# A two-layer trunk kernel whose list scheduler gets other delays and another plan for the front parts

## The chip, the cores and the metric

The kernel runs on one core of one Trainium2 chip. The metric is the device time of one execution in microseconds (us). The engines of the core are TensorE (PE in the profile), VectorE (DVE), ScalarE (ACT), GpSimd (POOL) and SyncE (SP). SyncE only issues transfers (DMAs); POOL issues some too.

## The reference, cut to what matters

Sequence length 512, model width 1024, two layers, everything in float32:

```python
h = x @ w_in[l]                                  # 1024 -> q | k | v | u, 512 each
q, k, v, u = jnp.split(h, splits, axis=-1)
attn_out = diff_attention(q, k, v, lam, ...)     # rotary, 4 heads, two softmaxes each, p0 - lam * p1, RMSNorm per head
ssm_out = s5_ssm(u, ...)                         # 32 groups of 16 channels, 64 complex states each, GELU, GLU
mix = jnp.concatenate([attn_out, ssm_out], axis=-1) @ w_out[l]
x = layer_norm(ALPHA * x + mix, ln1_g[l], ln1_b[l])
ff = jnp.square(jax.nn.relu(x @ w_ff1[l])) @ w_ff2[l]    # 1024 -> 4096 -> 1024
x = layer_norm(ALPHA * x + ff, ln2_g[l], ln2_b[l])
```

## The kernel before, in words

**Products.** Every float32 product is three products in a faster format (`mm3`): both factors are split in a high part and the rest, and high x high, high x low and low x high are added up in PSUM. A weight tile of 128 x 1024 comes by DMA into `raw`; `whi` is a ScalarE cast of it, `wlo` the difference `raw - whi`. Who makes `wlo` is chosen by a letter in `PLAN` (lines 42 to 85): V is one VectorE subtraction, P one GpSimd subtraction, A a ScalarE activation with scale -1 and then a DMA from POOL's queue that adds `raw` on its way. The strings are `lo` (projections, one letter per tile in the order of `back`), `flo` (first feed-forward matrix), `nlo` (out-projection), `glo` (second feed-forward matrix) and `elo` (the last feed-forward block). There are four buffers of `whi` and of `wlo` and five of `raw`.

**Stages, with their time in the profiled execution.** The front of layer 0 (0 to some 216 us) holds the projections (groups `0q0` to `0q3`, `0k0`.., `0v0`.., `0u0`..), four attention heads of four row blocks (`0a00` to `0a33`, each head finished in `0e0` to `0e3`), the state-space model in four quarters (`0ssm_pars`, `_load`, `_a`, `_b`, `_c`, `_outp`) and the GLU (`0g0` to `0g3`). The out-projection and LayerNorm follow, then the feed-forward loop (267 to 556 us). Layer 1 has the same: its front from 556 to 780, its loop from 820 to 1117, and the last block with the store up to the end. The tables of layer 1's state-space model are made inside layer 0.

**Part-height copies.** The input of the state-space model is spread over partitions with 16 ScalarE copies of 32 x 128 per quarter (`u<-ps_acc`), its output matrices with 32-row copies too (`mx<-m`). q and k go through ScalarE casts of 64 x 512 (`xq<-rt`) and four 32-row DMAs for the rotary halves (`rt<-rt`).

**The feed-forward loop.** Each of seven blocks runs `f m1 m7 f m2 m4 f m6 f m5 m3`: `f` is a tile of the first matrix (24 products of 512 columns, then on ScalarE the ReLU `rt`, on VectorE the square, into `y` or `mh`), m1 to m7 are the seven products of a Strassen-like scheme over the second matrix (12 products each, in two PSUM banks `ps_sc`; VectorE adds each bank into `xq` or `rt`). m5 and m3 share their two banks, so m3's first product into a bank waits until m5's result was added from it. The eighth block (`ffend`) is an ordinary product.

**What sets the order.** The kernel first records all instructions (`Rec.add`), with their dependences. `cost` says how long each holds its engine, `lat` how much later one that depends on it can start. `run` is a list scheduler: it simulates the engines and at each step takes, on the engine that is free first, the ready instruction with the smallest `prio`, which is minus the longest path to the end (`rank`) minus an offset. The offsets come from stage knobs (`ao`, `ap` for attention, `so`, `sp` for the state-space model, `po` for layer 1's tables) and from the table `pri`, two numbers per group, the first for all engines but TensorE and the second for TensorE. Where the simulated TensorE would idle for more than 500 ns ahead of an attention head's work, `fill` puts filler products of 256 columns on a constant (`ps_sc<-wz`), whose result is never read. At the end `issue` emits everything in planned order, so all instructions of the profile have one line, L506. The chip then runs each engine's list in that order, whatever the true durations are.

Of the kernel before, what the change touches and what calls it, by code (L numbers as in the profile page):

```python
# [14 lines left out]
F32R = mybir.dt.float32r  # L15
# [5 lines left out]
P = 128  # L21
# [22 lines left out]
        "q0 u0 k0 u1 v0 u2 v1 q1 k1 u3 q2 v2 k2 v3 q3 k3 g0 g1 g2 g3".split(),  # L44
        "u0 k0 u2 q0 u1 v0 v1 q1 k1 u3 v2 q2 k2 v3 q3 k3 g0 g1 g2 g3".split(),
    ],
    "att": [[8, 11, 14, 18], [8, 12, 15, 18]],
    "s5": [[4, 14], [3, 13]],
    "bufs": {"slot": 13, "mh": 2, "y": 3, "xq": 13, "at": 4, "rt": 5, "u": 4},
    "ps": {"acc": 2, "sc": 4, "s5": 2},  # L50
    "lo": ["AAAVAAPAAAAVAAAAAAAA", "AAAAAAAAAAAAAAAVAAVA"],
    "eng": {"rope": ["VVV", "VVV"], "tab": ["VVVVVV", "VVVVVV"], "cg": ["VVVV", "VVPV"], "ch": ["VVVV", "VVVV"], "sa": ["PV", "VP"], "sb": ["VVVVVV", "VVVVVV"]},
    "flo": "AVVV",
    "nlo": "APVAVPPV",
    "glo": "VPPPAPV",
    "seq": "f m1 m7 f m2 m4 f m6 f m5 m3",
    "elo": "VVVV",
    "wb": 4,
    "s5o": "p1 p0 o0 a0 b0 a1 c0 p2 o1 b1 a2 c1 b2 p3 a3 o2 b3 c2 o3 c3",
    "swq": "S",  # L60
    "ao": [-6000, 4000],
    "so": [2000, 19000],
    "ap": [40500, 56750],
    "sp": [31000, 27000],
    "pw": -6000,
    "smk": 2,
    "raw": 5,
# [110 lines left out]
class Rec:  # L178
# [181 lines left out]
    def run(self):  # L360
# [4 lines left out]
        todo, rel, wait = {}, {}, {}  # L365
# [26 lines left out]
        while len(order) < len(self.ops):  # L392
            best = None
            for e in engs:
                if ready[e]:
                    t = free[e]
                elif future[e]:
                    t = max(free[e], future[e][0][0])
# [6 lines left out]
            t, e = best  # L405
# [27 lines left out]
            if op.port:  # L433
                t = max(t, port["POOL" if e == "DVE" else "DVE"])
# [4 lines left out]
            if e == "PE" and t - pe_end > PLAN["gap"][1]:  # L439
                n = self.fill(pe_end, t, warm, live, extra)  # L440
# [1228 lines left out]
```

## Time and profile before

| | |
|---|---|
| median of 3 timed runs | 1150.72 us (1150.34 to 1151.69) |
| the profiled execution | 1151.48 us, of which the profile's span is 1149.7 |
| mean granted TensorE clock | 0.997 of full |
| TensorE busy | 1117.1 us, 97% |
| VectorE busy | 912.5 us, 79% |
| ScalarE busy | 632.2 us, 55% |
| GpSimd busy | 260.3 us, 23% |

Times within the trace are us from the start of the span. A figure in brackets behind an instruction is the idle time of its engine ahead of it and what ended that.

### The profile page before, as it was taken

What the parts mean: (1) busy time and instruction counts of PE and PEld (TensorE: products, weight loads), DVE (VectorE), ACT (ScalarE), POOL (GpSimd) and SP (SyncE); (2) the same over time, 40 slices, a digit from 0 to 9 for tenths busy, and PEclk for the clock granted to TensorE, in tenths of its full rate; (3) what the DMA queues carried; (4) which work ended last, traced back from release to release, by engine and by line L of the source; (5) the groups of instructions that cost most, each with busy time, mean ns of one, the idle gap of its engine ahead of it and who ended that gap; (6) DMA issues with size and microseconds to landing.
All of it is one profiled execution on the core that took longest, in us unless ns stands there. A gap on an engine that the chain in (4) does not pass through costs nothing.

```text
span 1149.7 us, 16190 instructions
## 1 busy us (share of the span) xinstructions
PE 1117.1 (97%) x5840; PEld 936.0 (81%) x5840; DVE 912.5 (79%) x1569; ACT 632.2 (55%) x1202; POOL 260.3 (23%) x198
## 2 busy tenths in 40 slices
PE   9999999999999999999999999999999999999997
PEld 7778877889888888888788878878988888888885
DVE  7898998887778878767792988867777778778788
ACT  7886869425544464444537788873454445445440
POOL 1011110311232242133021221022032143133221
PEclk9999999999999999999999999999999999999999
DMA  9443642441562452553678662652444454355231
GB/s 320 101 119 75 156 121 65 157 135 58 147 155 86 129 168 86 147 147 99 197 202 216 173 169 63 191 155 79 137 139 123 134 128 129 110 147 129 91 110 74
DMA packets 50960, 154.12 MB, mean 134 GB/s; under 512 B 6848, under 2 KB 7104, under 8 KB 50880
## 3 DMA queue, kind: packets, MB, share of 16 engines
q1 hardware_dynamic: 42240, 121.63, 32.6%
q0 software_dynamic: 8640, 31.46, 15.3%
q8 instruction: 46, 0.75, 0.3%
q14 instruction: 34, 0.28, 0.1%
HBM read 110.07 MB, written 7.34 MB: 102 GB/s over the span
## 4 chain that ended last, share of the span: by engine, by line
PE 66%; ACT 5%; DVE 2%; issue 2%; DMA 1%; SPq 0%; DVEq 0%; ACTq 0%; POOLq 0%
PE ps_acc L506 35%; PE ps_sc L506 23%; PE ps_s L506 8%; ACT whi L506 1%; ACT u L506 1%; DVE xq L506 1%; DVE wlo L506 1%; ACT at L506 1%; ACT wlo L506 1%; DMA wlo<-raw 0%; DMA keep<-xq 0%; ACT xq L506 0%; ACT xTh L506 0%; DVE xTl L506 0%; DMA xq<-xs 0%
## 5 line engine op out<-in xcount | busy, mean ns | idle before, releaser
L506 ACT CAST whi<-raw 128x1024 fp32r<-128x1024 f32 x222 | 232.2, 1051 | 264.2 <-PE ps_acc L506 129.4
L506 PE MATMUL ps_acc<-xTh,whi 128*128 128x512 f32 (+1 forms) x712 | 268.9, 379 | 4.6 <-ACT u L506 3.7
L506 PE MATMUL ps_acc<-xTl,whi 128*128 128x512 f32 (+1 forms) x712 | 268.3, 378 | 1.7 <-DVE xTl L506 1.3
L506 PE MATMUL ps_acc<-xTh,wlo 128*128 128x512 f32 (+1 forms) x712 | 268.0, 378 | 0.0
L506 PE MATMUL ps_sc<-whi,slot 128*128 128x512 f32 x784 | 254.5, 391 | 1.2 <-DVE xq L506 0.6
L506 POOL TENSOR_TENSOR wlo<-raw,whi 128x1024 fp32r<-128x1024 f32 x62 | 156.2, 2519 | 418.7 <-ACT whi L506 410.9
L506 PEld LDWEIGHTS ps_sc<-whi,slot 128*128 128x128 f32 x784 | 147.0, 188 | 34.6 <-issue 4.1
L506 DVE TENSOR_TENSOR wlo<-raw,whi 128x1024 fp32r<-128x1024 f32 x100 | 122.0, 1221 | 47.1 <-ACT whi L506 47.0
L506 PEld LDWEIGHTS ps_acc<-xTh,whi 128*128 128x128 f32 x712 | 134.0, 188 | 29.3 <-ACT u L506 4.5
L506 PEld LDWEIGHTS ps_acc<-xTl,whi 128*128 128x128 f32 x712 | 134.1, 188 | 24.7 <-DVE xTl L506 1.9
L506 PE MATMUL ps_sc<-wlo,slot 128*128 128x512 f32 x392 | 153.0, 390 | 0.0
L506 PEld LDWEIGHTS ps_acc<-xTh,wlo 128*128 128x128 f32 x712 | 133.9, 188 | 22.9 <-DMA wlo<-raw 0.3
L506 DVE TENSOR_TENSOR slot<-slot 128x512 fp32r<-128x512 f32 (+4 forms) x143 | 126.5, 893 | 6.5 <-ACT slot L506 6.0
L506 POOL DMA_DIRECT2D wlo<-raw x60 | 53.0, 887 | 231.5 <-ACT wlo L506 114.6
L506 ACT ACTIVATE wlo<-raw 128x1024 fp32r<-128x1024 f32 x60 | 63.4, 1059 | 61.9 <-PE ps_s L506 32.4
L506 PEld LDWEIGHTS ps_sc<-wlo,slot 128*128 128x128 f32 x392 | 73.6, 188 | 14.7
L506 DVE TENSOR_TENSOR xq<-xq,ps_sc 128x512 f32<-128x512 f32 x124 | 83.1, 679 | 0.7 <-PE ps_sc L506 0.7
L506 DVE TENSOR_TENSOR raw<-raw 128x1024 f32<-128x1024 f32 x56 | 68.4, 1221 | 0.6
L506 ACT CAST slot<-slot 128x512 fp32r<-128x512 f32 x56 | 34.5, 617 | 51.1 <-DVE slot L506 49.1
L506 PE MATMUL ps_acc<-whi,xTh 128*128 128x256 f32 (+1 forms) x176 | 56.4, 320 | 0.8 <-ACT u L506 0.7
L506 PE MATMUL ps_acc<-wlo,xTh 128*128 128x256 f32 (+1 forms) x176 | 55.9, 319 | 0.4 <-DVE wlo L506 0.4
L506 PE MATMUL ps_acc<-whi,xTl 128*128 128x256 f32 (+1 forms) x176 | 55.4, 318 | 0.0
(229 smaller groups left out, 1902.3 us busy)
## 6 DMA issues: line engine op xcount, KB each, us to landing
raw<-in_w_ff_dram SPq DMA_DIRECT2D x128, 512.0 KB, 3.5
wlo<-raw POOLq DMA_DIRECT2D x60, 512.0 KB, 5.3
raw<-in_w_qk_dram SPq DMA_DIRECT2D x16, 512.0 KB, 5.2
raw<-in_w_out_dram SPq DMA_DIRECT2D x16, 512.0 KB, 4.1
raw<-in_w_u_dram SPq DMA_DIRECT2D x8, 512.0 KB, 5.4
raw<-in_w_v_dram SPq DMA_DIRECT2D x8, 512.0 KB, 6.6
rt<-rt SPq DMA_DIRECT2D x64, 64.0 KB, 2.6
at<-in_ln_dram SPq DMA_DIRECT2D x16, 256.0 KB, 4.4
```

Of the source, the lines that this page charges most:

```text
L506: getattr(self.real[op.eng], op.name)(*[_real(x) for x in op.a], **{n: _real(x) for n, x in op.k.items()})
```

## The change

Two things. The numbers of `lat`, `cost` and `run` change: a ScalarE result is seen by POOL after 180 ns (395 when POOL issues a DMA on it) in place of 140; part-height copies cost 113 ns more on ScalarE and 105 more on VectorE; SP's DMAs hold the queue for 690 or 520 ns in place of 650 or 475; plain float32 products 10 ns of overhead in place of 5; products with an `xq` operand get a spacing of their own; `accum_out` on ScalarE 130 in place of 95; two GpSimd forms have new formulas; and ScalarE waits 80 ns after a buffer was released. And the plan changes: the letters of some low halves, the engine of a state-space combination of layer 1 (`cg`, one of four from GpSimd to VectorE), the stage knobs, and 71 of the 92 entries of `pri`, which gets 17 new ones (two of them are shown, the others read alike).

```diff
-    "att": [[8, 11, 14, 18], [8, 12, 15, 18]],
-    "s5": [[4, 14], [3, 13]],
+    "att": [[8, 12, 15, 19], [8, 12, 15, 18]],
+    "s5": [[4, 14], [6, 13]],
...
-    "eng": {..., "cg": ["VVVV", "VVPV"], ...},
+    "eng": {..., "cg": ["VVVV", "VVVV"], ...},
...
-    "nlo": "APVAVPPV",
-    "glo": "VPPPAPV",
+    "nlo": "APVAVPVP",
+    "glo": "APVPAPV",
     "seq": "f m1 m7 f m2 m4 f m6 f m5 m3",
-    "elo": "VVVV",
+    "elo": "AVVV",
...
-    "s5o": "p1 p0 o0 a0 b0 a1 c0 p2 o1 b1 a2 c1 b2 p3 a3 o2 b3 c2 o3 c3",
+    "s5o": "p1 p0 o0 a0 b0 a1 c0 p2 o1 b1 a2 b2 c1 p3 o2 a3 b3 c2 o3 c3",
...
-    "ao": [-6000, 4000],
+    "ao": [-6000, 20000],
...
-    "ap": [40500, 56750],
-    "sp": [31000, 27000],
+    "ap": [52500, 80750],
+    "sp": [31000, 29000],
...
-    "po": 2000,
+    "po": -6000,
...
-    "pri": {"1a30": [-2000, -16000], "1q1": [12000, 18000], ...},
+    "pri": {"1a30": [7000, 10000], "1q1": [22000, 34000], ...},
...
+        if a == "ACT" and b == "POOL":
+            return 395.0 if op.name == "dma_start" else 180.0
...
-            return (650.0 if o.p[1] - o.p[0] == 32 else 475.0) if e == "DMA" else 1030.0, 1550.0 + 1.35 * op.move
+            return (690.0 if o.p[1] - o.p[0] < 128 else 520.0) if e == "DMA" else 1030.0, 1550.0 + 1.35 * op.move
...
-                return max(c * 4, 213.0) + 5.0, 0.0
+                return max(c * 4, 213.0) + 10.0, 0.0
+            if r.dt == F32R and r.t.key[1] == "xq":
+                return max(c + {256: 35.0, 384: 50.0, 512: 42.0}.get(o.idx.size, 13.2), 116.0), 0.0
...
-            return 67.0 + n / 0.96, 0.0
+            p = o.p[1] - o.p[0] < P or any(v.t.space != "DRAM" and v.p[1] - v.p[0] < P for _, v in views)
+            return 67.0 + n / 0.96 + 105.0 * p, 0.0
...
-            t = (45.0 if s else 90.0) + n / 1.2 + (95.0 if "accum_out" in op.k else 0.0)
+            t = (45.0 if s else 90.0) + n / 1.2 + (130.0 if "accum_out" in op.k else 0.0)
+
+            t += 113.0 * (o.p[1] - o.p[0] < P)
...
-            return 38.0 + n / 1.2, 0.0
+            return max(170.0, 38.0 + n / 1.2), 0.0
+        if op.name == "tensor_copy":
+            return 50.0 + n / 1.05, 0.0
...
-                start = max(start, rel[v.key][0])
+                start = max(start, rel[v.key][0] + (80.0 if e == "ACT" else 0.0))
```

What this makes of the instructions, counted in the two orders:

| engine | before | after |
|---|---|---|
| TensorE products | 5536 | 5520 (the 16 are fillers: 168, then 152) |
| fillers between `0u1` and `0v0` / ahead of `0q1` / in the later part of front 0 | 12 / 0 / 115 | 63 / 8 / 40 |
| low halves on VectorE / ScalarE and POOL DMA / GpSimd | 100 / 60 / 62 | 98 / 76 / 48 |
| combinations `u<-u` on VectorE / GpSimd (of the kind that `cg` chooses) | 4 / 4 | 8 / 0 |
| SP's DMAs | 338 | 338, in another order: the load of the rotary table stands ahead of both `0v0` weight loads, in place of between them |

VectorE in the feed-forward loop of layer 1, the end of a block. `rt`, `xq` from `ps_sc` are evacuations of m1..m7, `mh` the square of an `f` tile, `raw` the sums of weight blocks. Before:

```order
L506 TENSOR_TENSOR rt<-rt,ps_sc 128x512 x2
L506 TENSOR_TENSOR raw<-raw 128x1024 x2
L506 TENSOR_TENSOR wlo<-raw,whi 128x1024
L506 TENSOR_TENSOR xq<-xq,ps_sc 128x512
L506 TENSOR_TENSOR mh<-rt,ps_acc 128x2x256
L506 TENSOR_TENSOR xq<-xq,ps_sc 128x512
```

And now:

```order
L515 TENSOR_TENSOR rt<-rt,ps_sc 128x512 x2
L515 TENSOR_TENSOR raw<-raw 128x1024 x2
L515 TENSOR_TENSOR xq<-xq,ps_sc 128x512
L515 TENSOR_TENSOR mh<-rt,ps_acc 128x2x256
L515 TENSOR_TENSOR xq<-xq,ps_sc 128x512
L515 TENSOR_TENSOR slot<-mh,y 128x512
L515 TENSOR_TENSOR xq<-xq,ps_sc 128x512
L515 TENSOR_TENSOR wlo<-raw,whi 128x1024
```

The low half of the next m1's weights no longer stands ahead of the evacuations of m5 (the first two `xq`); the next low half on VectorE stands behind the first evacuation of m3 or later.

TensorE in the front of layer 1, the second quarter of the state-space model (`ps_s<-u,slot`) among value projections (`ps_acc<-`). Before:

```order
L506 MATMUL ps_s_6303<-u,slot 128x128
L506 MATMUL ps_acc<-wlo,xTh 128x256
L506 MATMUL ps_acc<-whi,xTl 128x256
L506 MATMUL ps_s_6303<-u,slot 128x128
L506 MATMUL ps_acc<-whi,xTh 128x256
L506 MATMUL ps_acc<-wlo,xTh 128x256
L506 MATMUL ps_acc<-whi,xTl 128x256
L506 MATMUL ps_s_6303<-u,slot 128x128
```

And now:

```order
L515 MATMUL ps_s_6304<-u,slot 128x128
L515 MATMUL ps_acc<-whi,xTl 128x256
L515 MATMUL ps_acc<-whi,xTh 128x256
L515 MATMUL ps_acc<-wlo,xTh 128x256
L515 MATMUL ps_acc<-whi,xTl 128x256
L515 MATMUL ps_acc<-whi,xTh 128x256
L515 MATMUL ps_acc<-wlo,xTh 128x256
L515 MATMUL ps_acc<-whi,xTl 128x256
L515 MATMUL ps_s_6304<-u,slot 128x128
```

Seven value products stand between two state products, in place of two or three. Between the end of `1u3` and `1q2` there are now 48 value products, in place of 37.

TensorE at the end of layer 0's front. `ps_sc<-cs,at` are the transposes of head 3's result, `whi,mh` and the first `whi,xTh` of the out-projection belong to the parts of `mix` that are ready, the last `whi,xTh` here to head 3. Before:

```order
L506 MATMUL ps_sc<-cs,at 128x128 x2
L506 MATMUL ps_acc<-whi,xTl 128x512
L506 MATMUL ps_sc<-cs,at 128x128
L506 MATMUL ps_acc<-whi,mh 128x512
L506 MATMUL ps_s_2536<-whi,mh 128x512
L506 MATMUL ps_s_2526<-wlo,mh 128x512
L506 MATMUL ps_acc<-whi,mh 128x512
L506 MATMUL ps_s_2536<-whi,mh 128x512
L506 MATMUL ps_s_2526<-whi,mh 128x512
L506 MATMUL ps_acc<-whi,xTh 128x512
```

And now:

```order
L515 MATMUL ps_acc<-wlo,xTh 128x512
L515 MATMUL ps_s_2469<-wlo,xTh 128x512
L515 MATMUL ps_acc<-whi,xTl 128x512
L515 MATMUL ps_s_2469<-whi,xTl 128x512
L515 MATMUL ps_sc<-cs,at 128x128 x4
L515 MATMUL ps_acc<-whi,xTh 128x512
```

Six products stood between the last transpose and head 3's first out-projection product; now there is none.

## Rows read from the trace of the kernel before

**Rows 1.** The page: busy time, share of the span and instructions of each engine.

```profile
PE 1117.1 (97%) x5840; PEld 936.0 (81%) x5840; DVE 912.5 (79%) x1569; ACT 632.2 (55%) x1202; POOL 260.3 (23%) x198
```

**Rows 2.** By stage: length; PE, PEld, DVE, ACT, POOL busy; clock; DMA share, GB/s.

```profile
45.00:216.00 171.00, 161.48 (x1007) 134.75 (x1005) 152.15 (x363) 129.00 (x342) 28.25 (x35) 0.99 0.42 110
...
600.00:780.00 180.00, 174.68 (x1119) 151.07 (x1118) 131.76 (x265) 136.81 (x344) 32.08 (x39) 1.00 0.61 163
820.00:1117.00 297.00, 295.84 (x1341) 244.72 (x1341) 228.61 (x276) 140.84 (x178) 81.62 (x41) 1.00 0.44 123
```

**Rows 3.** The same table for fillers: PE, PEld, DVE, clock, DMA.

```profile
25.00:45.00 20.00, 1.48 (x12) 1.09 (x12) 0.00 (x0) 1.00 0.69 174
140.00:216.00 76.00, 13.18 (x110) 10.58 (x110) 0.00 (x0) 0.98 0.38 111
```

**Rows 4.** TensorE's waits, 45 to 216 us: total, count, longest.

```profile
PE ps_s L506 <- ACT mx L506: 2.8, 2, 1.6
PE ps_acc L506 <- ACT u L506: 2.1, 2, 1.4
```

**Rows 5.** Timeline of layer 1's front: start, duration, instruction, idle ahead.

```profile
629.06 0.49 PE L506 MATMUL ps_s<-u,slot 128*128 128x128 f32 x2 [1.41 <-ACT u L506]
...
631.78 4.31 ACT L506 COPY u<-ps_acc 32x128 f32<-32x128 f32 x16 [0.21 <-PE ps_acc L506]
...
633.96 0.49 PE L506 MATMUL ps_s<-u,slot 128*128 128x128 f32 x2 [0.35 <-ACT u L506]
...
685.37 0.50 PE L506 MATMUL ps_acc<-xTh,whi 128*128 128x512 f32 x1 [1.60 <-ACT u L506]
```

**Rows 6.** Timeline of layer 1's feed-forward loop, the end of a block.

```profile
866.00 1.05 ACT L506 CAST whi<-raw 128x1024 fp32r<-128x1024 f32 x1 [3.43 <-issue]
866.96 0.58 ACT L506 ACTIVATE rt<-ps_acc 128x512 f32<-128x512 f32 x1
867.09 1.22 DVE L506 TENSOR_TENSOR wlo<-raw,whi 128x1024 fp32r<-128x1024 f32 x1 [3.23 <-ACT whi L506]
868.23 0.68 DVE L506 TENSOR_TENSOR xq<-xq,ps_sc 128x512 f32<-128x512 f32 x1
868.48 0.39 PE L506 MATMUL ps_sc<-whi,slot 128*128 128x512 f32 x1
869.06 0.47 PE L506 MATMUL ps_sc<-whi,slot 128*128 128x512 f32 x1 [0.19 <-DVE xq L506]
```

**Rows 7.** The chain that ended last: start, length, engine, instructions.

```profile
636.75 4.79 PE ps_acc L506 x40
...
872.04 5.44 PE ps_acc L506 x24
```

**Rows 8.** Low halves by form, 820 to 1117 us: ns min/median/max; ACT: busy, mean.

```profile
L506 POOL TENSOR_TENSOR wlo<-raw,whi x28: 2392/2411/3016, 837.2 to 1106.3; 128x1024 fp32r<-128x1024 f32 x28
L506 POOL DMA_DIRECT2D wlo<-raw x13: 874/874/890, 852.6 to 1100.3; - x13
DMA to landing us min/median/max: 4.5/4.6/5.9
L506 ACT ACTIVATE wlo<-raw 128x1024 fp32r<-128x1024 f32 x13 | 13.8, 1058 | 5.6 <-issue 3.7 <-PE ps_sc L506 1.9
```

**Rows 9.** Timeline of the start of layer 1's front.

```profile
567.83 0.39 PE L506 MATMUL ps_s<-idw,gx 128*128 128x144 f32 x1 [1.30 <-ACT idw L506]
```

**Rows 10.** Timeline of layer 0's first projections, TensorE.

```profile
39.72 0.50 PE L506 MATMUL ps_sc<-xq 128*128 128x128 f32 x2 [0.82 <-ACT xq L506]
```

**Rows 11.** Timeline of the end of layer 0's front, TensorE's weight loads.

```profile
217.85 0.19 PEld L506 LDWEIGHTS ps_acc<-whi,xTh 128*128 128x128 f32 x1 [0.37 <-ACT xTh L506]
```

**Rows 12.** Timeline of layer 0's front, the longest wait on `mx`.

```profile
158.19 0.49 PE L506 MATMUL ps_s<-mx,u 128*128 128x128 f32 x2 [1.63 <-ACT mx L506]
```

**Rows 13.** By stretch as in rows 2, around that wait.

```profile
156.00:160.00 4.00, 2.01 (x11) 1.58 (x10) 3.39 (x6) 3.83 (x13) 0.97 (x1) 0.85 0.21 75
160.00:164.00 4.00, 4.00 (x26) 3.57 (x25) 2.89 (x9) 1.95 (x9) 0.31 (x1) 0.72 0.00 0
```

More of the change, by code (lines that the diff above doesn't have):

```diff
@@ L51 @@
     "lo": ["AAAVAAPAAAAVAAAAAAAA", "AAAAAAAAAAAAAAAVAAVA"],
-    "eng": {"rope": ["VVV", "VVV"], "tab": ["VVVVVV", "VVVVVV"], "cg": ["VVVV", "VVPV"], "ch": ["VVVV", "VVVV"], "sa": ["PV", "VP"], "sb": ["VVVVVV", "VVVVVV"]},
+    "eng": {"rope": ["VVV", "VVV"], "tab": ["VVVVVV", "VVVVVV"], "cg": ["VVVV", "VVVV"], "ch": ["VVVV", "VVVV"], "sa": ["PV", "VP"], "sb": ["VVVVVV", "VVVVVV"]},
     "flo": "AVVV",
-    "nlo": "APVAVPPV",
-    "glo": "VPPPAPV",
+    "nlo": "APVAVPVP",
+    "glo": "APVPAPV",
     "seq": "f m1 m7 f m2 m4 f m6 f m5 m3",
-    "elo": "VVVV",
+    "elo": "AVVV",
     "wb": 4,
-    "s5o": "p1 p0 o0 a0 b0 a1 c0 p2 o1 b1 a2 c1 b2 p3 a3 o2 b3 c2 o3 c3",
+    "s5o": "p1 p0 o0 a0 b0 a1 c0 p2 o1 b1 a2 b2 c1 p3 o2 a3 b3 c2 o3 c3",
     "swq": "S",
-    "ao": [-6000, 4000],
+    "ao": [-6000, 20000],
     "so": [2000, 19000],
-    "ap": [40500, 56750],
-    "sp": [31000, 27000],
+    "ap": [52500, 80750],
+    "sp": [31000, 29000],
     "pw": -6000,
@@ L73 @@
     "pt": "u",
-    "po": 2000,
+    "po": -6000,
     "m3": 4,
-    "pri": {"1a30": [-2000, -16000], "1q1": [12000, 18000], "1v1": [0, 0], "0ssm_a0": [2000, 0], "0ssm_a1": [18000, 8000], "0ssm_a2": [9000, 8000], "0ssm_a3": [2000, 0], "0ssm_b0": [18000, -8000], "0ssm_b1": [2000, 0], "0ssm_b2": [2000, 0], "0ssm_b3": [5000, -8000], "0ssm_c0": [19000, 0], "0ssm_c1": [2000, 0], "0ssm_c2": [2000, 0], "0ssm_c3": [10000, 8000], "0ssm_outp0": [2000, 0], "0ssm_outp1": [2000, 0], "0ssm_outp2": [2000, 0], "0ssm_outp3": [2000, 0], "0ssm_pars0": [2000, 0], "0ssm_pars1": [4000, 0], "0ssm_pars2": [2000, 0], "0ssm_pars3": [2000, 0], "1a10": [17000, -10000], "0a10": [14000, -4000], "0a22": [2000, 0], "0q1": [-2000, 8000], "0q2": [-2000, 8000], "0q3": [-2000, 8000], "0g1": [0, 12000], "1ssm_outp3": [2000, -14000], "0u2": [18000, 8000], "0u3": [16000, 8000], "1a02": [20000, -12000], "1a31": [22000, -12000], "1a21": [12000, -6000], "1a03": [14000, -20000], "1a11": [14000, -20000], "1a13": [10000, -20000], "1a20": [-2000, -24000], "1a22": [-1000, -20000], "1a23": [14000, -14000], "1a32": [10000, -28000], "1a33": [14000, -20000], "1q3": [5000, 12000], "0k0": [24000, 12000], "0k2": [8000, 8000], "0k3": [8000, 8000], "1ssm_load2": [-3000, 8000], "1ssm_a0": [-4000, 0], "0g3": [6000, 16000], "0u0": [2000, 0], "0u1": [10000, 2000], "1u0": [3000, 12000], "1u2": [4000, 20000], "1e3": [24000, 24000], "1a01": [17000, 2000], "0q0": [8000, 8000], "0v0": [0, 16000], "0v1": [16000, 2000], "1e0": [1000, 0], "0v2": [12000, 16000], "0a12": [0, -8000], "0a01": [-1000, -8000], "0e1": [2000, -16000], "1ssm_b3": [-3000, -2000], "1e1": [0, 10000], "1g3": [8000, 0], "1g1": [1000, 0], "1ssm_b2": [-4000, -8000], "0a13": [2000, -4000], "1a00": [18000, -12000], "1a12": [2000, -16000], "1v3": [15000, -16000], "1e2": [-8000, 0], "1k2": [4000, 2000], "1ssm_outp1": [8000, -32000], "1ssm_a1": [-4000, 0], "1ssm_a2": [-4000, 0], "1ssm_a3": [-4000, 0], "1ssm_b0": [-4000, 0], "1ssm_b1": [-8000, 0], "1ssm_c0": [-4000, 0], "1ssm_c1": [-4000, 0], "1ssm_c2": [-4000, 0], "1ssm_c3": [-4000, 0], "1ssm_load1": [-4000, 0], "1ssm_load3": [-4000, 0], "1ssm_outp2": [-4000, 0], "0k1": [2000, 4000], "0v3": [8000, 16000], "0a31": [-2000, -4000]},
@@ new lines @@
+    "pri": {"1a30": [7000, 10000], "1q1": [22000, 34000], "1v1": [0, 0], "0ssm_a0": [2000, 0], "0ssm_a1": [21000, 2000], "0ssm_a2": [26000, 2000], "0ssm_a3": [2000, 0], "0ssm_b0": [16000, -8000], "0ssm_b1": [0, 4000], "0ssm_b2": [0, 8000], "0ssm_b3": [17000, -8000], "0ssm_c0": [19000, 0], "0ssm_c1": [2000, 0], "0ssm_c2": [4000, -2000], "0ssm_c3": [10000, 8000], "0ssm_outp0": [2000, 4000], "0ssm_outp1": [2000, 0], "0ssm_outp2": [2000, 0], "0ssm_outp3": [0, -8000], "0ssm_pars0": [2000, 0], "0ssm_pars1": [4000, 0], "0ssm_pars2": [10000, 4000], "0ssm_pars3": [2000, 0], "1a10": [20000, -38000], "0a10": [30000, 0], "0a22": [2000, -8000], "0q1": [-2000, 8000], "0q2": [-2000, 8000], "0q3": [-4000, 8000], "0g1": [-8000, 10000], "1ssm_outp3": [-15000, -10000], "0u2": [18000, 8000], "0u3": [16000, 8000], "1a02": [49000, -24000], "1a31": [37000, -8000], "1a21": [26000, -26000], "1a03": [43000, -32000], "1a11": [35000, -24000], "1a13": [21000, -34000], "1a20": [4000, -54000], "1a22": [7000, -34000], "1a23": [43000, 12000], "1a32": [21000, -24000], "1a33": [30000, 22000], "1q3": [21000, 16000], "0k0": [24000, 10000], "0k2": [8000, 8000], "0k3": [8000, 8000], "1ssm_load2": [0, 36000], "1ssm_a0": [-9000, 12000], "0g3": [6000, 26000], "0u0": [0, -6000], "0u1": [11000, -14000], "1u0": [3000, -4000], "1u2": [12000, 24000], "1e3": [24000, 24000], "1a01": [8000, 20000], "0q0": [2000, -4000], "0v0": [-2000, 20000], "0v1": [14000, 6000], "1e0": [9000, -4000], "0v2": [11000, 20000], "0a12": [8000, -8000], "0a01": [-1000, -8000], "0e1": [2000, -32000], "1ssm_b3": [-8000, 10000], "1e1": [2000, 20000], "1g3": [8000, 0], "1g1": [3000, -2000], "1ssm_b2": [-9000, 4000], "0a13": [3000, -8000], "1a00": [29000, 4000], "1a12": [32000, -44000], "1v3": [15000, -16000], "1e2": [-6000, 4000], "1k2": [12000, -2000], "1ssm_outp1": [4000, -12000], "1ssm_a1": [-9000, 12000], "1ssm_a2": [-9000, 12000], "1ssm_a3": [-5000, 28000], "1ssm_b0": [5000, 10000], "1ssm_b1": [-13000, 8000], "1ssm_c0": [-7000, 20000], "1ssm_c1": [-11000, 0], "1ssm_c2": [-7000, 28000], "1ssm_c3": [-1000, 0], "1ssm_load1": [-5000, 14000], "1ssm_load3": [15000, 16000], "1ssm_outp2": [-27000, 8000], "0k1": [6000, 4000], "0v3": [22000, 16000], "0a31": [-18000, -6000], "0a03": [-15000, 2000], "0a30": [-1000, -2000], "1g0": [0, 8000], "1q0": [17000, 12000], "1q2": [34000, 20000], "0a02": [1000, 4000], "1v2": [8000, -8000], "0e0": [0, -16000], "0e3": [2000, -24000], "0g0": [2000, 8000], "1k0": [4000, -2000], "1k1": [4000, -2000], "0g2": [-2000, -2000], "0a11": [2000, 2000], "1v0": [1000, 0], "0e2": [-2000, -4000], "0a33": [1000, 8000]},
```

## The prediction

> **What bounds the kernel now.** I read the share of each engine first. TensorE is busy 97% of the span, VectorE 79%, ScalarE 55% [rows 1]. So another order can win only what TensorE does not use, the idle 32.6 us (1149.7 - 1117.1), and what it spends on the filler products on the constant `wz`, whose result nobody reads. Next I read the table by stage [rows 2]: the front of layer 0 from 45 to 216 us has 9.5 us without TensorE work, the front of layer 1 (600 to 780) 5.3 us, the feed-forward loop of layer 1 (820 to 1117) only 1.2 us. Few fillers stand at 25 to 45 us (12, 1.48 us), most after 140 us (110, 13.18 us, 0.12 each) [rows 3]. Then I read what ends TensorE's waits in each stage, and last the timeline around these waits. In the fronts it is the part-height ScalarE copies: between 45 and 216 us `mx` ends 2.8 us of waits and `u` 2.1 us [rows 4], and `u` ends the largest waits of layer 1's front [rows 5]. In the loop it is one VectorE instruction in front of an evacuation [rows 6].
>
> **Term 1, feed-forward loop of layer 1.** In one block ScalarE casts the high half of the next weight tile (1.05 us), VectorE makes its low half (1.22 us, right behind the cast), and only then does VectorE evacuate m5's first bank, 868.23 to 868.91. m3's first product needs that bank and starts at 869.06; from the product ahead of it (868.48) that is 0.58 us, where the pace is 0.227 (5.44 / 24) [rows 6, 7]. The loss is 0.35 us. Seven blocks have it, from the one at 869.06 to the one at 1116.41, at 0.35 or 0.31 each: 2.3 us. The change takes this low half to ScalarE and a POOL DMA, so the evacuation no longer stands behind it. What is late next is m5's second bank: ScalarE now does cast, low half and then the ReLU `rt`, VectorE's square `mh` needs `rt`, and the second evacuation stands behind the square: 1.05 + 1.06 + 0.58 + 0.68 + 0.68 = 4.05 us (the square like an evacuation) from the start of m5, against 18 products x 0.227 = 4.09 us until m3 uses that bank. Just in time, so I count all: **-2.3 us**. Bounds: 0 (the second bank is late by as much) and -2.5.
>
> What is added for it: 14 low halves (m1, both layers) go from VectorE to ScalarE and a POOL DMA, and 14 (m3) from POOL to VectorE. ScalarE, busy 140.8 of 297 us, gets 7 x 1.06 = 7.4 us more; VectorE keeps its count; POOL loses 7 x 2.41 us and gains 7 issues of 0.87 us [rows 2, 8]. An m1 low half then takes cast 1.05, activation 1.06, issue 0.87 and 4.5 to 5.9 us from issue to landing, 7.5 to 8.9 us. Its buffers come free with the `f` tile four tiles earlier, so m5, m3 and the next `f`, (12 + 12 + 24) x 0.227 = 10.9 us, cover it. If the issue stands behind a POOL subtraction of 2.41 us, the sum is 9.9 to 11.3, level with the cover. I take 0 and keep +1 us a block for rival C.
>
> The Trainium skill (SBUF — State Buffer, section "SBUF: two separate sides") says that descriptors of a DMA issued by POOL cannot be written while VectorE holds the port pair that the two share, and gives about 3100 ns for a transfer of 620 ns. By it each m1 tile would come some 2.5 us later, an estimate from that page. The trace does not bear it out: the 13 issues of this kind in the loop took 874 ns at the minimum and the median and 890 at most, while VectorE was busy 228.6 of 297 us [rows 2, 8].
>
> **Term 2, front of layer 1.** Waits on `u`: 1.41 us (629.06), 0.35 (633.96) and two more of 0.25 like it, and 1.60 (685.37), together 3.86 us [rows 5]. Sixteen 32-row copies take 4.31 us, 0.27 each. The products of the second state group wait for four more of them each time, 1.07 us, and stand two or three value products apart (0.24 to 0.36 us). After the change seven stand between two of them: 7 x 0.12 + 0.22 = 1.06 us, what four copies need (0.12 is 4.79 / 40) [rows 5, 7]. Ahead of the wait at 685.37 stand eleven more value products, 11 x 0.12 = 1.3 of 1.60 us. That at 629.06 can go too, where a bank that sixteen copies had to release is now released by one. So up to 3.9 us can go, of 5.3 idle in that stage. But the whole list of priorities of this front is new, and a wait hidden so far may come out elsewhere; I take a little over half: **-2.2 us**, bounds -4.5 and +2.
>
> **Term 3, start of layer 1's front.** The largest wait there is 1.30 us for `idw` at 567.83 [rows 9]; two products of 0.23 more stand ahead of it, 0.46 us. Of the last feed-forward block one low half of four goes to ScalarE and a DMA that is made ahead of the block like the others. **-0.4 us**, bounds -1.1 and +0.5.
>
> **Term 4, front of layer 0.** Four parts. (a) Late fillers: 75 fewer, less 8 new ones ahead of `q1`: 67 x 0.12 = -8.0 us if real work takes their place, 0 if TensorE waits there instead. (b) Early fillers: 63 in place of 12 between `u1` and `v0`, 51 x 0.12 = +6.1 us. TensorE has little idle time there now, 0.82 us at most [rows 10], so they are cost, unless the second low half of `v0`, which is later in VectorE's order and whose load now stands behind the rotary table in the SP queue, opens a wait that they fill (0). I take the whole. (c) The tail: head 3's transposes had six products (1.36 us) between them and the out-projection's first product on head 3, whose weight load still waited 0.37 us for the cast `xTh` [rows 11]; after, none. Seven fewer stand ahead of the transposes, 1.6 us, and again ahead of that head's last exponential, where 1.2 us are not covered: +4.2. (d) The waits on `mx` and `u`, now planned with the length that the copies have: 4.9 us in all [rows 4], the largest 1.63 [rows 12]; I take half, -2.5. Sum: -8.0 + 6.1 + 4.2 - 2.5 = **-0.2 us**, bounds -5 and +5. VectorE is busy 152 of 171 us here [rows 2] and by the new order has 7 us more to do before head 3's end (5.6 us of layer 1's state tables, a low half of 1.22), so I see no large gain.
>
> One rule speaks against taking fillers away. The row first: after TensorE waited 1.63 us at 158.19, the granted clock is 0.85 and then 0.72 of full between 156 and 164 us, part of that time at 1.2 in place of 2.4 GHz; (0.15 + 0.28) x 4 = 1.7 us of work are lost [rows 12, 13]. The Trainium skill (TensorE: Matmul & The Clock Gate, section "Part 1: The HAM clock gate") says that the throttled state is the default and only activity releases it. The trace agrees, in one place of 171 us. Without 67 fillers there may be three such places, +3.4 us: part of rival B.
>
> **Sum.** -2.3 - 2.2 - 0.4 - 0.2 = -5.1 us. Against the profiled run, 1151.48 us (span 1149.7, and 1.8 around it), that gives 1146.4. That run lies 0.8 above the median of the three timed runs, 1150.72; with the same 0.8 taken off, **1145.6 us**.
>
> **The rivals.**
> - A, front 0 gives back more: (a) and (d) in full and (b) hidden, -8.0 - 4.9 + 4.2 = -8.7 in place of -0.2: 1137.1. For it: 13.2 us of late fillers and 9.5 us idle in one stretch. Against it: VectorE's 89%.
> - B, nothing comes of it: the early fillers are pure cost, and where the late ones stood TensorE waits, in part at the low clock. Term 4 at +4.5, sum -0.4: 1150.3. For it: VectorE's 89% and the row on the clock. Against it: the waits on part-height copies are real and are what the new order was given.
> - C, slower: in the 14 blocks the m1 low half lands after m1's products could begin, because its issue stands behind a POOL subtraction. It decides once the sum passes 10.9 us; at 11.3 and three signals of 0.15 (868.91 to 869.06) a block loses 0.9, and 14 blocks 12 us: 1158. Against it: seven subtractions fewer per loop, and the present 13 tiles of this form make no wait.
> - D, slower: VectorE ends front 0. Its 7 us more before head 3 move the end by 7, and half of the tail (2.1) stands behind it: -4.9 + 9.1 = +4.2, 1155. It decides if VectorE has no gap left before head 3; it has 19 us of gaps now, nearly all waits for others.
>
> **How the numbers follow.** Forecast, own range 1141 to 1148.4: 0.53. A 0.13, B 0.18, C 0.07, D 0.09. A measurement can tell 0.2%, 2.3 us, from no change, so the edges are 1148.4 and 1153.0. Faster: forecast, A and a little of B, 0.67. Same: most of B and some of D, 0.18. Slower: C and the rest of D, 0.15. The range reaches to A's near side and past B: 1138 to 1152.
>
> **What would show it.** Right: in the changed profile m3's first product starts 0.23 us after the one ahead of it in all seven blocks; no wait on `u` over 1 us is left between 600 and 780; the last loop takes 2 us less. C would show as a TensorE wait on the DMA `wlo<-raw` once a block. For front 0, head 3's first out-projection product (217.85 now) tells the cases apart: about 217.5 by the forecast, 209 in A, 222 in B, 227 in D. The forecast is wrong if the front of layer 1 is not shorter, or if that product moves by over 5 us.

## The result, and the profile after

| | before | after |
|---|---|---|
| median | 1150.97 us (1150.34 to 1151.69, 4 runs) | 1134.57 us (1133.23 to 1134.81, 4 runs) |
| ratio | | 0.9855, 95% interval 0.9838 to 0.9872 |
| profiled execution, its span | 1151.48, 1149.7 | 1134.35, 1132.3 |

The change makes the kernel 16.4 us faster. The forecast was 1145.6 with a range of 1138 to 1152: right in sign, a third of the size, and the time lies below the range, beyond even rival A (1137.1).

The engines of the changed kernel, then its stages (length; PE, PEld, DVE, ACT, POOL busy; granted clock; DMA share, GB/s), each cut some 10 to 17 us earlier than in [rows 2] because everything ends earlier:

```profile
PE 1107.5 (98%) x5824; PEld 931.9 (82%) x5824; DVE 912.9 (81%) x1571; ACT 646.4 (57%) x1218; POOL 235.8 (21%) x196
```

```profile
45.00:206.00 161.00, 155.11 (x967) 130.25 (x966) 154.41 (x355) 127.67 (x333) 26.10 (x33) 1.00 0.45 115
590.00:765.00 175.00, 173.24 (x1119) 150.88 (x1120) 131.61 (x263) 136.82 (x344) 32.15 (x39) 1.00 0.64 167
805.00:1100.00 295.00, 294.85 (x1344) 245.64 (x1343) 229.60 (x276) 148.24 (x187) 70.57 (x42) 1.00 0.53 138
```

VectorE has as much to do as before (912.9 us, 912.5 in [rows 1]) but less time for it. In layer 0's front it is busy 154.41 of 161 us, 96%, where [rows 2] had 89%. The front of layer 1 has 1.8 us without TensorE work in place of 5.3.

Four marks are the same in every trace: the first TensorE instruction (1.38 us), the first m1 product of layer 0's loop, that of layer 1's loop, and the last loop product there (`ps_sc<-whi,slot`). Their distances tell where time went. What is lost in a stretch shows when the pace of its products (0.227 us for 512 columns, 0.120 for 256, and so on) is taken off its length:

| stretch | before | after | difference | forecast |
|---|---|---|---|---|
| start to first m1 of layer 0 (front 0, out-projection, first `f` tiles) | 277.69 | 268.84 | -8.85 | -0.2 (term 4) |
| to first m1 of layer 1 (loop 0, front 1) | 557.01 | 550.95 | -6.06 | -2.6 (terms 2, 3) |
| to the last of layer 1's loop | 282.93 | 280.41 | -2.52 | -2.3 (term 1) |

The middle distance holds two gains. Counted that way, some 5.0 us of the 6.06 were gained in layer 1's front and 0.9 in layer 0's loop, for which the prediction has no term.

The second mark, before and after (start, duration, instruction):

```profile
279.06 0.39 PE L506 MATMUL ps_sc<-whi,slot 128*128 128x512 f32 x1
```

```profile
270.22 0.39 PE L515 MATMUL ps_sc<-whi,slot 128*128 128x512 f32 x1
```

**Layer 1's loop** went as worked out. The end of a block in the timeline of the changed kernel, to be held against [rows 6]:

```profile
851.10 1.05 ACT L515 CAST whi<-raw 128x1024 fp32r<-128x1024 f32 x1 [3.43 <-issue]
852.06 1.05 ACT L515 ACTIVATE wlo<-raw 128x1024 fp32r<-128x1024 f32 x1
852.64 0.69 DVE L515 TENSOR_TENSOR xq<-xq,ps_sc 128x512 f32<-128x512 f32 x1 [3.25 <-PE ps_sc L515]
853.01 0.58 ACT L515 ACTIVATE rt<-ps_acc 128x512 f32<-128x512 f32 x1
853.40 0.87 POOL L515 DMA_DIRECT2D wlo<-raw  x1 [5.50 <-ACT wlo L515]
853.62 0.69 DVE L515 TENSOR_TENSOR mh<-rt,ps_acc 128x512 f32<-128x512 f32 x1 [0.29 <-ACT rt L515]
854.23 0.68 DVE L515 TENSOR_TENSOR xq<-xq,ps_sc 128x512 f32<-128x512 f32 x1
```

The first evacuation waits only for m5 now and is done 0.47 us before m3's first product (853.80, 0.227 us behind the one ahead of it). The second, behind cast, low half, ReLU and square, ends at 854.91, and m3 needs that bank six products after 853.80, at 855.16: in time by 0.25 us. Six of the seven blocks have no stall, the last has 0.31. No TensorE wait in the loop is put down to `wlo<-raw`, though landings took up to 7.1 us:

```profile
L515 POOL DMA_DIRECT2D wlo<-raw x21: 869/884/902, 813.0 to 1091.9; - x21
L515 POOL TENSOR_TENSOR wlo<-raw,whi x21: 2384/2410/3019, 822.3 to 1078.1; 128x1024 fp32r<-128x1024 f32 x21
DMA to landing us min/median/max: 4.5/4.7/7.1
```

So rival C's mechanism was not there. The Trainium skill (SBUF — State Buffer, section "SBUF: two separate sides") describes how a DMA issued by POOL is delayed while VectorE runs an operation in a two-port mode, such as a `tensor_copy`, and not a `tensor_tensor`. In this loop VectorE ran almost nothing but `TENSOR_TENSOR`, before and after, and the issues (869 to 902 ns, VectorE busy 229.6 of 295 us) show no delay, so the trace agrees. The 2.5 us a tile in the prediction came from applying that figure to instructions for which the skill does not give it.

**The waits** over the whole span (in all, times, longest). Before and after:

```profile
PE ps_acc L506 <- ACT u L506: 4.4, 5, 1.6
PE ps_s L506 <- ACT mx L506: 2.8, 2, 1.6
PE ps_sc L506 <- ACT at L506: 2.5, 6, 0.8
...
PE ps_s L506 <- ACT u L506: 2.0, 3, 1.4
```

```profile
PE ps_s L515 <- ACT mx L515: 2.9, 1, 2.9
...
PE ps_s L515 <- ACT u L515: 0.6, 1, 0.6
...
PE ps_sc L515 <- ACT at L515: 0.3, 1, 0.3
```

The listed waits on `u` fell from 6.4 to 0.6 us, those on `at` (attention) from 2.5 to 0.3. `mx` still has one of 2.9 us. This view does not list a wait in which fillers stand: the changed kernel has another of 7 us on `u`, from 30 to 37 us, under its early fillers (e3).

**Where front 0 gained.** I counted TensorE's real products (without fillers) as they began, each at its pace. At 140 us the changed kernel is behind, 112.9 us of work done against 118.1. From 140 to 190 the kernel before did only 26.1 us of work in 50, the changed one 41.3. That stretch held 12.0 us of fillers and 11.9 us that were neither filler nor product at its pace; now it is 4.4 and 4.3.

### The profile page after: what moved, and what is told of

Read it like the earlier page. It is cut to its first block, busy times and chain, and to the rows that moved or that the text cites. A ratio compares the mean times of both kernels' runs of the same rounds, so it can differ in the third digit from the quotient of the medians.

```text
span 1132.3 us, 16187 instructions
## 1 busy us (share of the span) xinstructions
PE 1107.5 (98%) x5824; PEld 931.9 (82%) x5824; DVE 912.9 (81%) x1571; ACT 646.4 (57%) x1218; POOL 235.8 (21%) x196
## 4 chain that ended last, share of the span: by engine, by line
PE 44%; ACT 3%; issue 1%; DMA 1%; DVE 1%; SPq 0%; POOL 0%; DVEq 0%; ACTq 0%; POOLq 0%
PE ps_acc L515 23%; PE ps_sc L515 14%; PE ps_s L515 7%; DMA wlo<-raw 1%; ACT at L515 1%; ACT whi L515 1%; DMA slot<-keep 0%; ACT xTh L515 0%; ACT wlo L515 0%; DVE xq L515 0%; ACT xq L515 0%; ACT mx L515 0%; DVE wlo L515 0%; ACT jk L515 0%; ACT hx L515 0%
## 5 line engine op out<-in xcount | busy, mean ns | idle before, releaser
L515 PE MATMUL ps_sc<-whi,slot 128*128 128x512 f32 x784 | 251.2, 390 | 0.1
L515 POOL TENSOR_TENSOR wlo<-raw,whi 128x1024 fp32r<-128x1024 f32 x48 | 121.1, 2523 | 231.3 <-ACT whi L515 183.4
L515 DVE TENSOR_TENSOR wlo<-raw,whi 128x1024 fp32r<-128x1024 f32 x98 | 119.5, 1221 | 56.3 <-ACT whi L515 54.6
L515 POOL DMA_DIRECT2D wlo<-raw x76 | 66.9, 881 | 400.1 <-ACT wlo L515 190.0
L515 ACT ACTIVATE wlo<-raw 128x1024 fp32r<-128x1024 f32 x76 | 80.3, 1059 | 70.3 <-PE ps_s L515 32.3
```

The source lines that it names most:

```text
L515: getattr(self.real[op.eng], op.name)(*[_real(x) for x in op.a], **{n: _real(x) for n, x in op.k.items()})
```

## The experiments

The distances are those of the table above (front 0 / loop 0 and front 1 / loop 1), of the one profiled execution of each kernel, which lies up to 2.8 us from its median (e8); times are medians, ratios against the kernel before on the same chip with their 95% interval.

| kernel | us | ratio | distances | listed waits on `u` |
|---|---|---|---|---|
| before | 1151 | | 277.7 / 557.0 / 282.9 | 6.4 |
| after | 1134.57 | 0.9855 (0.9838, 0.9872) | 268.8 / 551.0 / 280.4 | 0.6 |
| e1 new plan, old delays | 1164.09 | 1.0114 (1.0100, 1.0127) | 286.5 / 563.1 / 281.4 | 9.4 |
| e2 old plan, new delays | 1140.00 | 0.9906 (0.9893, 0.9920) | 272.5 / 550.0 / 282.9 | none listed |
| e5 old plan, one new delay | 1145.59 | 0.9952 (0.9937, 0.9966) | 269.7 / 559.0 / 283.2 | 0.4 |
| e14 old plan, two new delays | 1141.22 | 0.9913 (0.9897, 0.9929) | 268.7 / 556.2 / 283.0 | 0.6 |
| e11 old plan, all delays but one | 1160.72 | 1.0086 (1.0071, 1.0101) | 284.1 / 562.0 / 282.9 | 9.1 |
| e6 after, without that one | 1157.36 | 1.0054 (1.0039, 1.0069) | 278.3 / 565.2 / 280.4 | 9.3 |
| e9 old plan, new delays and letters | 1139.59 | 0.9899 (0.9882, 0.9915) | 274.7 / 551.5 / 280.4 | none listed |
| e12 after, old letters | 1138.67 | 0.9893 (0.9877, 0.9908) | 270.0 / 549.9 / 282.9 | 0.7 |
| e7 before, new `glo` | 1151.37 | 1.0002 (0.9993, 1.0011) | 277.5 / 559.4 / 280.8 | 6.6 |
| e8 delays, layer 0's plan new | 1142.36 | 0.9920 (0.9903, 0.9936) | 271.9 / 556.2 / 282.9 | none listed |

The theory: the old planner gave the part-height copies too little time, so it put behind them what could not start, and the order that it made waited on the chip; right numbers alone repair that. The main rival: letters and priorities bring the gain.

**e1 and e2, the two halves of the change.** e1 has the new `PLAN` in the old kernel, e2 the old `PLAN` in the new one.

> The new plan (letters, knobs, priorities) scheduled with the old delays. Theory 'delays': the gain comes from the order being made with the lengths that part-height copies have, so the same plan with the old lengths loses most of it: 1142 to 1150 us, with TensorE waits on u or mx of over 1 us back. Rival 'plan': the letters and priorities bring it by themselves: 1134 to 1138 us.

> The old plan scheduled with the new delays. Theory 'delays': a third or more of the 16 us is there: 1138 to 1146 us, the waits on u in the front of layer 1 (3.9 us before) mostly gone. Rival 'plan': nothing or a loss, 1149 to 1156 us, since the offsets were set for other lengths.

The delays alone give 11.2 us of the 16.4. The plan alone costs 12.9: neither theory had it slower than before. Here a plan was good only with the delays that it was set with. The waits of e1:

```profile
PE ps_acc L506 <- ACT u L506: 7.2, 5, 2.5
PE ps_sc L506 <- ACT at L506: 6.1, 8, 1.5
PE ps_s L506 <- ACT u L506: 2.2, 1, 2.2
```

**e5, e6, e11 and e14, which delay.** e5 adds one line to the kernel before, e6 takes it out of the changed kernel, e11 out of e2, and e14 adds VectorE's number too.

```diff
+            t += 113.0 * (o.p[1] - o.p[0] < P)      # ScalarE: e5, e14 add it, e6, e11 take it out
+            return 67.0 + n / 0.96 + 105.0 * p, 0.0 # VectorE: e14
```

By the old formula a 32 x 128 copy out of PSUM holds ScalarE for 45 + 128 / 1.2 = 152 ns; with the line it is 265; in [rows 5] sixteen take 4.31 us, 269 each. Copies of full height do come as fast as the old formula says: two of 128 x 128 out of PSUM, 0.27 us each, take 0.43, so the second begins 0.16 us behind the first:

```profile
561.47 0.43 ACT L506 COPY xq<-ps_s 128x128 f32<-128x128 f32 x2
```

The line reaches every ScalarE instruction on fewer than 128 partitions: 128 copies into `u`, 48 into `mx`, 64 of 64 x 256 (`gx`, `hx`) and the 48 casts of 64 x 512. No run takes these apart.

> The kernel before with one number changed: part-height ScalarE instructions cost 113 ns more in the planner. Theory 'one number' (it is the length of these copies): at least half of what all new delays together gave (11.2 us) is there: 1139 to 1145 us, and the waits on u at 629, 634 and 685 us are gone. Rival 'all together': the other numbers (queue spacing, signals to POOL, waits after a release) are needed too: 1146 to 1155 us.

> The changed kernel with this one number taken out again. Theory 'one number': most of the gain is lost, since the plan's offsets rest on it as well: 1145 to 1165 us, waits on u or mx of over 1 us come back. Rival 'all together': it keeps more than half of the gain, under 1142 us.

> The old plan with all new delays but the 113 ns of part-height ScalarE instructions. That number alone gave 5.8 us, all together 11.2. Theory 'two halves': the others bring the rest, some 5 us: 1144 to 1148 us. Rival 'only with it': without it they give nothing or a loss: 1149 to 1158 us.

> The kernel before with two numbers: 113 ns for part-height ScalarE and 105 ns for part-height VectorE instructions. The first alone gave 5.8 us, all new delays 11.2, all but the first a loss of 9.8. Theory 'part height': the other part of the gain is the same thing on the second engine: 1139 to 1142.5 us. Rival 'other numbers': queue spacing and signals matter as much: 1143.5 to 1149 us.

This number is the one that carries the rest. Every kernel of the table that has it has 0.7 us or less of listed waits on `u`, every kernel without it 6.4 or more. Alone it gives 5.8 us (1145.59, just outside the range of its theory and of the rival), and 8.0 in front 0, of which loop 0 and layer 1 take back 2.0 and 0.3. With VectorE's number front 0 is as short as in the changed kernel (268.7) and the total is 10 us below the kernel before: of the two theories, part height. All the other delays without it lose 9.8 us (e11), more than either theory had: half-right numbers were worse than the old ones. Chance is a rival to each single run, since any new number makes a new order, and two letters alone move the second distance by 2.4 us (e7). But all seven kernels of the table with the number are faster than before, and the four changed ones without it are level or slower. The waits of e11:

```profile
PE ps_acc L514 <- ACT u L514: 9.1, 6, 3.4
PE ps_s L514 <- ACT mx L514: 2.8, 2, 1.6
```

In e5 what remains in front 0 is on `mx` and attention, and `u` has nearly gone:

```profile
PE ps_sc L507 <- ACT at L507: 2.7, 5, 1.0
PE ps_s L507 <- ACT mx L507: 2.3, 2, 1.6
...
PE ps_acc L507 <- ACT u L507: 0.4, 1, 0.4
```

**e7, e9 and e12, the letters.** e7 sets only `"glo": "APVPAPV"` in the kernel before; e9 puts `glo`, `nlo`, `elo` and `cg` into e2; e12 puts the old `glo` and `elo` into the changed kernel.

> The kernel before with the new letters for m1 and m3 of the second feed-forward matrix, nothing else. Theory (term 1): the seven stalls in front of m3 in layer 1's loop go by the letters alone, the loop from m1's first product to m3's last one takes 280.4 in place of 282.9 us; the fronts keep their waits, so 1147 to 1150.5 us. Rival: the stall is made by the old delays in the order, and the loop stays at 282.5 to 283.

> The old plan with all new delays and with the new letters (glo, nlo, elo, cg), but the old knobs and offsets. Alone the new delays gave 1140.0, the letters m1 and m3 alone nothing. Theory 'letters': with the delays right, the loop of layer 1 keeps its 2.1 to 2.5 us: 1137 to 1138.5 us. Rival 'given back': the start of layer 1's front takes it again, as with the letters alone: 1139.5 to 1142 us.

> The changed kernel with the old letters for the feed-forward matrices (glo VPPPAPV, elo VVVV). Theory 'letters': only the loop of layer 1 gets longer, by 2.5 us: 1136.5 to 1138 us. Rival 'chance': the fronts move too, by several us either way, because the offsets were set with the new letters: over 1139.

The letters do for layer 1's loop what term 1 says: 280.4 to 281.4 us wherever they are new (281.4 in e1), 282.9 to 283.2 wherever they are old. But in e7 and e9 the other parts grow by as much or more (2.4 us in the second distance in e7; 2.1 and 1.5 in the first two distances in e9, against e2), so the total stands still, against the 1147 to 1150.5 expected of e7. In e12 the total is 4.1 us above the changed kernel's, more than the loop's 2.5; its profiled execution, 1136.63, was the fastest of four (up to 1140.41), so where the rest lies that trace cannot tell. 1138.67 lies between the ranges of both theories.

**e8, the plan by layers.** It has the new delays, layer 0's new knobs and offsets, the new order string `s5o`, which both layers share, and all else of the old plan. Against the words of the expectation the letters were the old ones too.

> The changed kernel (new delays, new letters) with the stage knobs and offsets of layer 1's front as they were before. Theory 'delays suffice there': the front of layer 1 is as short as in the changed kernel, since the old plan with the new delays had no wait on u over 0.5 us there: 1132 to 1136 us. Rival 'plan': layer 1's new offsets are worth 3 us or more: 1137 to 1143 us.

1142.36 us is 2.4 above e2, whose plan is wholly old. Layer 0's new offsets give nothing by themselves (front 0 271.9 against 272.5), and the second distance is 6.2 us longer. That trace overstates it: its execution, 1145.11, was the slowest of four, and that of e2 the fastest. So the new offsets do not add up from parts either. How much of the missing 8 us is the letters', this run does not tell.

**e3 and e4, the fillers.** Order as it is, without 71 fillers of the changed kernel (e3: the 63 at 30 to 38 us and the 8 ahead of `0q1`, which stand at 71) or 115 late ones of the kernel before (e4):

```diff
-        order += extra
+        order += extra[:23] + extra[94:]   # e3;  e4: extra[:35]
```

> The changed kernel in the same order, without the 71 filler products that stand between u1 and q1 (7 us of TensorE at 28 to 45 us). Theory 'cost' (the prediction's): they hold up real products, so 6 to 8.5 us go: 1126 to 1129 us. Rival 'cover': they stand in a wait that is there anyway: 1133.5 to 1136 us and TensorE idle some 7 us between 28 and 45. Second rival 'clock': without them TensorE falls to 1.2 GHz there and it is slower than 1136.

> The kernel before in the same order, without the 115 filler products after 138 us. Theory 'cover': they stood in waits, real work was not ready: 1149 to 1152 us, and TensorE idle some 13 us more between 140 and 216. Rival 'cost': they held up real work: 1138 to 1145 us. Rival 'clock': TensorE falls to 1.2 GHz more often than at the one place before, 1153 to 1160 us.

e3: 1134.63 us, ratio 0.9862 (0.9847, 0.9878); e4: 1151.46, 1.0004 (0.9996, 1.0013). Neither changes anything: fillers stand in waits that are there anyway. The wait that they cover in the changed kernel is 7.1 us, for the two quarters' `u` copies with q casts among them:

```profile
37.62 0.58 PE L516 MATMUL ps_acc<-whi,xTh 128*128 128x256 f32 x1 [7.10 <-ACT u L516]
```

In e4 the waits under the late fillers come out, and they are on attention (140 to 200 us; the kernel before lists 0.4 us on `at` there):

```profile
PE ps_sc L507 <- DVE at L507: 8.2, 2, 4.7
PE ps_sc L507 <- ACT at L507: 2.7, 5, 1.4
```

The granted clock did fall without the fillers. e3 from 30 to 50 us, then e4 from 150 to 180 (columns as in the stages above):

```profile
30.00:40.00 10.00, 2.90 (x14) 2.48 (x13) 9.32 (x35) 8.89 (x25) 0.00 (x0) 0.77 0.53 168
40.00:50.00 10.00, 10.00 (x69) 9.07 (x69) 9.94 (x42) 5.81 (x16) 0.86 (x1) 0.89 0.48 106
```

```profile
150.00:160.00 10.00, 5.29 (x24) 4.23 (x24) 9.78 (x23) 7.95 (x21) 0.58 (x1) 0.83 0.53 163
160.00:170.00 10.00, 5.81 (x38) 4.28 (x36) 8.64 (x22) 4.90 (x18) 0.76 (x2) 1.00 0.26 86
170.00:180.00 10.00, 7.10 (x28) 5.80 (x29) 9.20 (x20) 6.38 (x18) 0.05 (x1) 0.56 0.16 53
```

In e4 TensorE works for 18.2 of 30 us, in part at 1.2 GHz, and the end does not move; VectorE is busy for 27.6 of these 30. The Trainium skill (TensorE: Matmul & The Clock Gate, section "Part 1: The HAM clock gate") says that a throttled clock follows from too little activity. The rows agree (0.56 from 170 to 180 us, 1.00 there in the kernel before), but what it costs depends on whether TensorE is the engine waited for: here it was not.

**e10 and e13, an attempt to beat both.** In ScalarE's order the last four `u` copies go ahead of four q casts; e10 has no early fillers, e13 keeps 36 of the 63 and the 8 ahead of `0q1` (27 are out; the count in its expectation is muddled).

> The changed kernel without its 71 early fillers, and with the last four of the 32-row copies of u1 ahead of four q casts in ScalarE's order, where they stood behind them. Without the fillers TensorE waited 7.1 us for these copies, up to 37.6 us. Theory 'order on ScalarE': the wait ends some 2 us earlier and the end follows: 1132 to 1133.5 us. Rival 'VectorE': what comes behind (rotary sums on VectorE and the first head) sets the pace, 1134 to 1136 us.

> The changed kernel with the four 32-row copies ahead of the q casts as in the run before, but with 36 of the 63 early fillers kept (44 of 71 taken out or, of the 8 ahead of q1, all 8 out). Without fillers the granted clock was 0.65 at 30 to 40 us and 0.84 at 40 to 50, some 5 us of TensorE work. Theory 'clock': with the fillers in the shortened wait of 4.4 us the clock stays at 1.00 and the earlier copies pay: 1131 to 1133.3 us. Rival 'VectorE': the clock stays at 1.00 but VectorE, busy 97% from 60 us on, sets the pace: 1134 to 1136.5 us.

e10: 1136.32, 0.9872 (0.9857, 0.9887); e13: 1136.12, 0.9871 (0.9855, 0.9888); above the changed kernel (0.9855) by 1.8 and 1.6 us, or by nothing, as the intervals overlap. The wait for the copies fell from 7.1 us to 4.4 in e10, and another came a few products later, on VectorE's rotary sums, which stand behind the casts that had to stand back (e13):

```profile
36.88 1.40 DVE L524 TENSOR_TENSOR xq<-rt,xq 64x512 fp32r<-64x512 f32 x2 [0.73 <-ACT xq L524]
...
40.27 0.44 PE L524 MATMUL ps_sc<-xq 128*128 128x128 f32 x2 [2.52 <-DVE xq L524]
```

So the earlier copies do not decide, which is the rivals' answer. The clock fell in both (0.65 and 0.84 of full in e10 from 30 to 50 us, 1.00 and 0.83 in e13, where both theories had 1.00 throughout), so e13 does not test it alone; e3 does, and there it cost nothing. That VectorE sets the pace, with ScalarE's order only choosing what waits, fits these rows but is not shown by itself. No kernel tried is faster than the changed one; e3 and it are level.

## Why the prediction was wrong

**Term 1 (-2.3):** right in place, mechanism and size: -2.52, and the letters alone do it (e7, e9, e12). That the next link is "just in time" held by 0.25 us. m3's first product starts 0.227 us after the one ahead of it in six of the seven blocks. The same place cost 0.14 to 0.19 us in five blocks of layer 0's loop (the first at 312.05), 0.9 in all; this went too, already in e2 with the old letters, and no term had it.

**Term 2 (-2.2):** the mechanism was right, the size was not. I found 3.9 us of waits on `u` and took a little over half, for fear that the new priorities would bring waits elsewhere. 3.3 us of them went (0.58 is left, at 622.87, so none over 1 us), and of 1.1 us on attention (0.80 and 0.31 on `at` at 664.80 and 707.27) 0.8. Counted against the products' pace the front gave about 5.0 us, beyond my bound of -4.5. Halving a wait because the order is new was no estimate from a row.

**Term 3 (-0.4):** nothing. The 1.30 us on `idw` went, and 1.51 came at the same products, so the listed waits around the start of layer 1's front are 3.0 us before (556 to 600) and 3.3 after (546 to 590):

```profile
558.50 0.76 PE L515 MATMUL ps_s<-idw,gx 128*128 128x144 f32 x4 [1.51 <-ACT xq L515]
```

**Term 4 (-0.2 in place of -8.85):** the step that failed. By the prediction's own sign it was wrong as well: head 3's first out-projection product moved by 6.1 us, from 217.85 to 211.79, which lies between the forecast (217.5) and rival A (209). Part by part:
- (a) The late fillers went as counted (-8.0 forecast, 75 fewer), and real work took their place. That was possible because the waits under them went; taking the fillers alone away gives nothing (e4).
- (b) I charged the early fillers with 6.1 us of TensorE time. e3 shows that they cost nothing; the wait under them does, and by 140 us the kernel is 5.2 us behind. So a cost of this size is there, but taking fillers away does not return it.
- (c) The tail was mis-sized: the product behind head 3's cast waits 0.78 us ([rows 11] had 0.37 for its weight load), and the time beyond the products' pace, from the start of the out-projection to the loop, grew from 2.0 to 3.5 us, by 1.5 and not 4.2.
- (d) Here lies most of the error, in a size. I took half of the 4.9 us of listed waits on `mx` and `u`. Between 140 and 200 us the time that is neither filler nor product at its pace went from 12.2 to 4.5 us, 7.7 less, more than the whole list. The list has 5.0 of the 12.2 (2.8 on `mx`, 0.7 on `hx`, 0.4 on `at`) and 1.4 of the 4.5. The clock, 0.97 of full from 140 to 190 us before and 1.00 now, makes some 1.7 us of the difference, and 2.4 no view names. I also did not see what the late fillers stand in, 10.9 us of waits on attention (e4). That a late copy makes the attention behind it late is argued, not shown link by link; shown is that one number for the part-height instructions moved front 0 by 8.0 us (e5).

The parts add up to -8.0 + 5.2 + 1.5 - 7.7 = -9.0. Rival A's -8.7 for this term comes as close by luck: it had (b) at nothing, (c) at 4.2 and (d) at 4.9.

Behind it stands a wrong reading of the bound. I held VectorE's 89% and its 7 us of additional work to be a limit ("no large gain"), and made rival D of it. But 19 us of its time were gaps, most of them waits for ScalarE (4.6 us on attention's `at`, 2.4 on `jk`, 1.9 on `rt`, 1.8 on the `u` copies) and 2.5 for the rotary DMAs; under 1 us was for TensorE. The changed kernel fills most of them: 96%. A busy share shows a limit only after its gaps have been read.

What the trace cannot yet tell is how the last 5.4 us between e2 and the changed kernel are made up. Layer 1's loop accounts for 2.5, by the letters. Front 0 is 3.7 shorter and the second distance 1.0 longer; there letters and offsets act on each other (e8, e9, e12), and no run takes them apart into single effects.

## What to carry to other kernels

Where a planner writes the order, compare its durations with the trace form by form before anything else: part-height ScalarE instructions planned 113 ns too short were worth 5.8 us alone, as much as all new letters and priorities on top of the new delays (5.4), and these priorities with the old delays were a loss. Correct the largest deviation first: a partial correction without it was slower than none. A list of waits is short by those in which fillers stand; a run without the fillers names them. And filler work, or a slower clock, cost nothing here where TensorE was not the engine waited for.

## What was not expected of the hardware

TensorE at a granted clock of 0.56 for 10 us (e4) left the end where it was; VectorE was busy for 9.2 of them. POOL's accumulating DMAs landed up to 7.1 us after their issue in the changed loop, against 5.9 before, with 21 in place of 13 of them; the cover of 10.9 us was enough. A 32 x 128 ScalarE copy out of PSUM holds the engine longer than a 128 x 128 one: the next begins 0.27 us behind it (4.31 us for sixteen), and 0.16 behind the copy of full height.
